# Modulation vectors in four column tiles of the array, and the first gate's products beside the first attention's preparation

## The chip, the cores and the metric

The kernel runs on one core of one Trainium2 chip. The metric is the time of one execution on the device in microseconds (us), the median of the runs shown. A core has five engines with a queue each: TensorE (PE in the profile, its weight loads PEld), VectorE (DVE), ScalarE (ACT), GpSimd (POOL) and SyncE (SP, which here only issues DMAs). Each engine works through its own list in order; semaphores make one wait for another.

## The reference, cut to what matters

Two blocks work on 1024 tokens and 256 context tokens of 1024 channels. Each layer is modulated by vectors that are computed from one conditioning vector `c` (for the tokens) and one `c_ctx` (for the context). The first block has two layers, with three vectors of 1024 each; the second block one layer with six:

```
# first block, layer l
shift, scale, gate       = split(silu(c)     @ w_mod[l] + b_mod[l], 3)
shift_c, scale_c, gate_c = split(silu(c_ctx) @ w_mod[l] + b_mod[l], 3)
h = rms_norm(x, norm_w[l]) * (1 + scale) + shift        # hc alike, from the context
parts = split_in(h @ w_in[l])
... attention, short convolution, conformer branch -> y ...
x = x + gate * (y @ w_out[l])
# second block
sh1, sc1, g1, sh2, sc2, g2 = split(silu(c) @ ada_w + ada_b, 6)     # and the same with c_ctx
u = layernorm(x) * (1 + sc1) + sh1
... SSD, RWKV and GLA mixers, then a mixture of experts ...
```

So `scale` and `shift` are wanted before a layer begins, and the gates only at its output projection.

## The kernel before, in words

`gemv` (L149 to L169) computes one such product for both vectors at once. `cs` holds silu(c) and silu(c_ctx) as 128 x 8 x 2: eight slices of 128 channels, two columns each. The matrix is read in chunks of 128 columns: one DMA on SP's queue brings a chunk `gemv_w` of 1024 x 128 (512 KB) into one of four buffers (two in the RWKV loop). Eight matmuls (L159), one per slice, add up to a result of 2 x 128 in PSUM: `cs[:, kk]` (128x2) is the stationary operand and the chunk's slice (128x128) the moving one. They are in fp32, and each appears as two records in the trace, so a chunk has 16 records. After four chunks (a group; two in the RWKV loop) VectorE copies the row of 2 x 512 to SBUF (L163), TensorE turns each 128 columns of it into 128 x 2 by a transpose (L166), and VectorE adds the bias (L168). `gemv` is a generator: it yields after each chunk, so its callers can put pieces of it between other work.

There are 96 chunks. Four places run them:

- `begin` in `block1`: layer 0's modulation (24 chunks). It runs all of shift and scale (16 chunks, four groups) and then `g` = (1 + scale) * norm_w (L398, L399). Then it goes through ten token tiles: `put_h` transposes a normalised tile (L248), scales and shifts it (L253 on VectorE, L256 on ScalarE) and splits it into two parts `hh` (L258) and `hl` (L259), two halves for each tile. After each tile one chunk of the gate runs (`run(gv, 1)`). The input projection (`product`, L104 to L106, three matmuls for each weight and token slice) follows.
- `second`, which `attention` of layer 0 gets as its `side`: layer 1's modulation (24 chunks). `beside(main, side, n)` runs `n` pieces of the side for each step of the main work, here while the first pair of heads is prepared: `prepare` (products, norms with a power on GpSimd at L87 and L847), `turn` (transposes of keys and queries, L876) and `maxima` (scores, L891, and their row maxima, L892 to L900). `run(side)` then finishes what is left of the side, and the attention's own first scores follow.
- the side of layer 1's attention: the second block's shift and scale (16 chunks of `ada_w`).
- the RWKV loop of the second block: the other 32 chunks of `ada_w`, with `group=2` and two buffers of `gemv_w`; there the PSUM tag `gv` has one bank, which the product and the transposes share.

The order of the instructions on each engine is fixed when the kernel is built, by a scheduler that goes by the program's order and the pools' free buffers. So an instruction of TensorE that waits holds up all that stands behind it on that engine.

The experts' loop at the end gathers rows by indices `ix`, of which the pool holds eight buffers, one for each block in flight.

Of the kernel before, what the change touches and what calls it, by code (L numbers as in the profile page):

```python
# [20 lines left out]
P = 128  # L21
# [18 lines left out]
class K:  # L40


    def __init__(self, ctx, tc):
# [12 lines left out]
        nc.vector.memset(ones, 1.0)  # L56
        self.ones = ones
        self.mhalf = self.const.tile([P, 1], F32, name="mhalf")
        nc.vector.memset(self.mhalf, -0.5)
# [84 lines left out]
def vec(ap):  # L144

    return ap.rearrange("(n p) -> n p", p=P)


def gemv(k, pool, out, cs, w, b, ncols, chunk=128, group=4, tag="mm", ttag="tr", bufs=4):  # L149

    nc = k.nc
    for g0 in range(0, ncols, chunk * group):
        ps = k.bank(tag=tag)
        n = min(chunk * group, ncols - g0)
        for c0 in range(0, n, chunk):
            wt = pool.tile([P, KD, chunk], F32, name="gemv_w", tag="gemv_w", bufs=bufs)
            k.load(wt, w[:, g0 + c0:g0 + c0 + chunk].rearrange("(k p) n -> p k n", p=P))
            for kk in range(KD):
                nc.tensor.matmul(ps[:2, c0:c0 + chunk], cs[:, kk], wt[:, kk], start=kk == 0, stop=kk == KD - 1)  # L159
            if c0 + chunk < n:  # L160
                yield
        row = pool.tile([2, chunk * group], F32, name="gemv_r", tag="gemv_r", bufs=2)
        nc.vector.tensor_copy(row[:, :n], ps[:2, :n])  # L163
        pt = k.bank(tag=ttag)
        for j in range(n // P):
            nc.tensor.transpose(pt[:, 2 * j:2 * j + 2], row[:, j * P:(j + 1) * P], k.ident[:2, :2])  # L166
        j0, nj = g0 // P, n // P
        nc.vector.tensor_tensor(out[:, j0:j0 + nj, :], pt[:, :2 * nj].rearrange("p (j s) -> p j s", s=2),  # L168
                                b[:, j0:j0 + nj].unsqueeze(2).to_broadcast([P, nj, 2]), op=OP.add)  # L169
        yield  # L170
# [153 lines left out]
def mod_vectors(k, pool, name, cvec, cctx):  # L324
    v = k.vectors(pool, name, [("c", vec(cvec)), ("cc", vec(cctx))])
    cs = pool.tile([P, KD, 2], F32, name=name + "_cs")
    sg = pool.tile([P, KD, 2], F32, name=name + "_sg")
    for s, key in enumerate(("c", "cc")):
        nc = k.nc
        nc.scalar.activation(sg[:, :, s], v[key], AF.Sigmoid)  # L330
        nc.vector.tensor_tensor(cs[:, :, s], sg[:, :, s], v[key], op=OP.mult)
    return cs


def block1(k, I, x_open, x_out, ahead, fill):
# [5 lines left out]
    with ExitStack() as es:  # L341
# [25 lines left out]
        def vectors(l):  # L367
# [20 lines left out]
            layer.append((v, hw, tabs))  # L388

        def modulation(l, gp, **kw):  # L390

# [3 lines left out]
            mods.append((m, g))  # L395
            n = 2 * KD
            yield from gemv(k, gp, m, cs, I["w_mod"][l], v["bmod"], 2 * D, **kw)
            nc.vector.tensor_scalar(g, m[:, KD:2 * KD], 1.0, None, op0=OP.add)  # L398
            nc.vector.tensor_tensor(g, g, v["norm"].unsqueeze(2).to_broadcast([P, KD, 2]), op=OP.mult)  # L399
            yield  # L400
            yield from gemv(k, gp, m[:, n:], cs, I["w_mod"][l][:, 2 * D:], v["bmod"][:, n:], D, **kw)

        def second(gp, **kw):

            vectors(1)
            yield from modulation(1, gp, **kw)

        hstack = ExitStack()
# [9 lines left out]
        def begin(wp):  # L418
# [15 lines left out]
            xs = [ready(t) for t in range(before)]  # L434
            run(gv, 2 * KD + 1 - 4)
            m, g = mods[0]
            for t in range(NT):
                s = 1 if t < CT else 0
                put_h(k, wp, xs[t], t, h[0], h[1], g[:, :, s], m[:, :KD, s])
                if t + before < NT:  # L440
                    xs.append(ready(t + before))
                run(gv, 1)
            run(gv)

# [708 lines left out]
class Mixer:  # L1153
# [1357 lines left out]
    def moe(self, xp, raw, late, finish):  # L2511
        k, nc, tc, I = self.k, self.nc, self.tc, self.I
        A = nc.vector
        with ExitStack() as es:
# [34 lines left out]
            def gather(st, pc, base):  # L2549
# [12 lines left out]
                A.scalar_tensor_tensor(c[:n, 0:1], c[:n, 2:3], slot[:n, 0:1], c[:n, 0:1], op0=OP.mult, op1=OP.add)  # L2562
                st.ix = xp.tile([P, 1], I32, name="ix", bufs=8)
                A.tensor_tensor(st.ix[:n], c[:n, 0:1], slot[:n, 1:2], op=OP.add)
# [342 lines left out]
```

## Time and profile before

| | us |
|---|---|
| median of 3 runs (4383.2 to 4387.87) | 4385.77 |
| profiled execution | 4396.88 |
| its span | 4394.7 |
| TensorE busy in it | 4042.7 (92%) |
| VectorE busy | 2889.0 (66%) |
| ScalarE busy | 1992.9 (45%) |
| GpSimd busy | 1172.9 (27%) |

The profile is of one execution. Busy time adds the records of an engine, and overlapping ones count once; matmuls are pipelined, so the mean of one record is longer than the distance from one start to the next. The clock granted to TensorE is 0.953 of full speed as a mean over the span. DMA moved 558.8 MB, at a mean of 127 GB/s.

### The profile page before, as it was taken

The page shows a single profiled execution, that of the slowest core. Times are in us where ns is not written, and L with a number is a line of the kernel's source. Part 1 is how long each engine was busy: PE and PEld are TensorE (multiplying, and loading weights), DVE is VectorE, ACT ScalarE, POOL GpSimd, SP SyncE. Part 2 cuts the span into 40 slices and gives each one's busy share as a digit, 9 for nine tenths or more (in the row PEclk, how much of TensorE's full clock was granted, in tenths as well). Part 3 has the DMA queues.
Part 4 walks back from the last instruction along what each step waited for, and adds up shares of the span by engine and source line. Part 5 has one row for each costly group of instructions (what it writes and reads, how often), then busy time and mean ns, then how long its engine had stood idle before and what let it go on. Part 6 is the DMA issues. An engine that isn't in the chain of part 4 may idle for free. (4 is left out here: it accounts for less than half of the span.)

```text
span 4394.7 us, 61923 instructions
## 1 busy us (share of the span) xinstructions
PE 4042.7 (92%) x22376; PEld 3080.2 (70%) x22376; DVE 2889.0 (66%) x5659; ACT 1992.9 (45%) x4292; POOL 1172.9 (27%) x1211
## 2 busy tenths in 40 slices
PE   8999899999998999999997999999999899899993
PEld 5787666667776666688786688777777666666662
DVE  4683577764745777645765555567878777777774
ACT  4122366653112666423353132434246666666664
POOL 1200133332101333321333331123312233222333
PEclk9999899999999999999997999799999999999996
DMA  6121400123123001334444410215359788888885
GB/s 187 34 64 41 126 13 13 30 80 107 44 63 106 8 13 37 110 121 127 125 126 137 123 34 27 83 34 173 113 211 300 249 274 270 259 264 260 272 264 166
DMA packets 371315, 558.80 MB, mean 127 GB/s; under 512 B 52126, under 2 KB 285056, under 8 KB 346048
## 3 DMA queue, kind: packets, MB, share of 16 engines
q1 hardware_dynamic: 335728, 432.81, 30.7%
q0 software_dynamic: 35280, 122.02, 10.7%
q8 instruction: 177, 2.90, 0.3%
q14 instruction: 130, 1.06, 0.1%
HBM read 438.42 MB, written 116.33 MB: 126 GB/s over the span
## 5 line engine op out<-in xcount | busy, mean ns | idle before, releaser
L95 DVE TENSOR_TENSOR wa_lo<-w_raw,wa_hi 128x512 fp32r<-128x512 f32 x520 | 340.2, 687 | 53.6 <-ACT wa_hi L94 51.0
L94 ACT ACTIVATE wa_hi<-w_raw 128x512 fp32r<-128x512 f32 x520 | 303.3, 625 | 90.8 <-PE mm L106 49.0
L104 PE MATMUL mm<-hh,w_hi 128*128 128x512 f32 (+1 forms) x848 | 319.3, 377 | 4.7 <-ACT h L256 4.7
L105 PE MATMUL mm<-hl,w_hi 128*128 128x512 f32 (+1 forms) x848 | 318.2, 375 | 0.0
L106 PE MATMUL mm<-hh,w_lo 128*128 128x512 f32 (+1 forms) x848 | 316.4, 373 | 0.0
L892 DVE TENSOR_REDUCE mx<-mm 128x1 f32<-128x512 f32 (+1 forms) x400 | 225.0, 587 | 53.4 <-PE mm L891 50.9
L926 ACT ACTIVATE pe<-mm 128x512 f32<-128x512 f32 (+1 forms) x336 | 193.0, 588 | 144.8 <-PE mm L106 115.6
L104 PE MATMUL mm<-wa_hi,xh 128*128 128x512 f32 (+3 forms) x632 | 257.6, 408 | 0.0
L105 PE MATMUL mm<-wa_lo,xh 128*128 128x512 f32 (+3 forms) x632 | 251.7, 398 | 1.2 <-DVE wa_lo L95 1.2
L106 PE MATMUL mm<-wa_hi,xl 128*128 128x512 f32 (+3 forms) x632 | 250.7, 397 | 2.1 <-DVE xl L95 2.1
L931 POOL TENSOR_TENSOR pl<-pe,ph 128x512 fp32r<-128x512 f32 x96 | 142.1, 1482 | 335.3 <-ACT ph L930 328.5
L931 DVE TENSOR_TENSOR pl<-pe,ph 128x512 fp32r<-128x512 f32 (+1 forms) x240 | 204.2, 863 | 38.6 <-ACT ph L930 37.3
L2629 POOL DMA_INDIRECT acc_d<-y,ix x97 | 171.3, 1766 | 201.7 <-DMA acc_d<-y,ix 86.9
L159 PE MATMUL mm<-gemv_w,b_c_cs 128*2 128x128 f32 x1536 | 197.3, 284 | 8.8 <-DMA gemv_w<-in_w_mod_dram 5.6
L595 DVE SCALAR_TENSOR_TENSOR acc<-zc,b_v,acc 128x512 f32<-128x512 f32 (+1 forms) x300 | 199.2, 711 | 1.5
L2585 PE MATMUL mm<-ident,xg 128*128 128x128 f32 (+5 forms) x840 | 119.4, 288 | 85.0 <-DMA xg<-h_d,ix 85.0
L104 PEld LDWEIGHTS mm<-hh,w_hi 128*128 128x128 f32 x848 | 160.9, 190 | 39.9 <-issue 7.6
L104 PE MATMUL mm<-wb_hi,hidh 128*128 128x512 f32 (+5 forms) x420 | 188.8, 450 | 0.0
L2585 PEld LDWEIGHTS mm<-ident,xg 128*128 128x128 f32 (+5 forms) x840 | 109.1, 198 | 111.2 <-issue 99.1
L2574 POOL COPY wc<-xg 128x1 f32<-128x1 f32 (+5 forms) x97 | 44.0, 454 | 534.6 <-DMA xg<-h_d,ix 534.6
L105 PEld LDWEIGHTS mm<-hl,w_hi 128*128 128x128 f32 x848 | 161.2, 190 | 34.3 <-issue 7.6
L94 ACT ACTIVATE w_hi<-w_raw 128x1024 fp32r<-128x1024 f32 x61 | 64.6, 1059 | 262.4 <-PE mm L105 227.6
(780 smaller groups left out, 11637.5 us busy)
## 6 DMA issues: line engine op xcount, KB each, us to landing
w_raw<-in_exp_w_dram SPq DMA_DIRECT2D x192, 1024.0 KB
w_raw<-in_w_in_dram SPq DMA_DIRECT2D x69, 512.0 KB
gemv_w<-in_w_mod_dram SPq DMA_DIRECT2D x48, 512.0 KB
gemv_w<-in_ada_w_dram SPq DMA_DIRECT2D x48, 512.0 KB
rec<-rec SPq DMA_DIRECT2D x64, 256.0 KB
wo_raw<-in_w_out_dram SPq DMA_DIRECT2D x20, 512.0 KB
y<-ydram SPq DMA_DIRECT2D x36, 256.0 KB
xt<-in_x_dram SPq DMA_DIRECT2D x16, 512.0 KB
```

What stands on the lines that cost most here:

```text
L94: nc.scalar.activation(hi, src, AF.Copy)
L95: eng.tensor_tensor(lo, src, f32(hi), op=OP.subtract)
L104: mm(out, ah, bh, start=start, stop=False)
L105: mm(out, ah, bl, start=False, stop=False)
L106: mm(out, al, bh, start=False, stop=stop)
L159: nc.tensor.matmul(ps[:2, c0:c0 + chunk], cs[:, kk], wt[:, kk], start=kk == 0, stop=kk == KD - 1)
L595: nc.vector.scalar_tensor_tensor(o, zc[:, ft, p0 + j:p0 + j + c[1]], v["cfw"][:, 2 * j + ft:2 * j + ft + 1], o, op0=OP.mult, op1=OP.add)
L892: nc.vector.tensor_reduce(mx[:, t, c:c + 1], ps[:, :n], axis=AX.X, op=OP.max)
L926: nc.scalar.activation(pe, ps, AF.Exp)
L931: (nc.gpsimd if j % PLP == PLP - 1 else nc.vector).tensor_tensor(pl, pe, f32(ph), op=OP.subtract)
L2585: nc.tensor.transpose(ps[:, j * n:(j + 1) * n], xk[:, 4 * q + j], k.ident[:n, :n])
L2629: nc.gpsimd.indirect_dma_start(out=self.acc_d, out_offset=bass.IndirectOffsetOnAxis(ap=st.ix[:n, 0:1], axis=0), in_=y[:n], in_offset=None, ...
```

## The change

The changed `gemv` widens the stationary operand. `gemv_c` is a zeroed tile of 128 x 8 x 32 with `cs` in its first two columns of each slice, made once per call. The eight matmuls of a chunk go to four column tiles of the array: slice `kk` writes to PSUM partitions 32 (kk mod 4) and up, so each tile adds up two slices, and the sum of the four tiles is still to be made. The row that VectorE copies now has 128 partitions (32 for each tile, two of them not zero) and one buffer in place of two. In place of each transpose four matmuls have 32 columns of that row as the stationary operand and `quads`, a constant of 128 x 2 with ones at the two rows of each tile, as the moving one: they sum the four tiles and turn the row at once, each into a column tile of its own.

The gate of layer 0 leaves `begin`; `second` runs it ahead of layer 1's vectors and modulation. So `begin` runs 16 chunks, and the side of the first attention 32. The buffers of `ix` are seven in place of eight.

```diff
+        self.quads = self.const.tile([P, 2], F32, name="quads")
+        nc.vector.tensor_reduce(self.quads, self.ident.rearrange("p (q s) -> p s q", q=4)[:, :2], axis=AX.X, op=OP.add)
...
     nc = k.nc
+    wide = pool.tile([P, KD, 32], F32, name="gemv_c", tag="gemv_c", bufs=1)
+    nc.vector.memset(wide, 0.0)
+    nc.vector.tensor_copy(wide[:, :, :2], cs)
...
             for kk in range(KD):
-                nc.tensor.matmul(ps[:2, c0:c0 + chunk], cs[:, kk], wt[:, kk], start=kk == 0, stop=kk == KD - 1)
+                q = slice(kk % 4 * 32, kk % 4 * 32 + 32)
+                nc.tensor.matmul(ps[q, c0:c0 + chunk], wide[:, kk], wt[:, kk], start=kk < 4, stop=kk >= KD - 4)
...
-        row = pool.tile([2, chunk * group], F32, name="gemv_r", tag="gemv_r", bufs=2)
-        nc.vector.tensor_copy(row[:, :n], ps[:2, :n])
+        row = pool.tile([P, chunk * group], F32, name="gemv_r", tag="gemv_r", bufs=1)
+        nc.vector.tensor_copy(row[:, :n], ps[:, :n])
         pt = k.bank(tag=ttag)
         for j in range(n // P):
-            nc.tensor.transpose(pt[:, 2 * j:2 * j + 2], row[:, j * P:(j + 1) * P], k.ident[:2, :2])
+            for q in range(0, P, 32):
+                nc.tensor.matmul(pt[q:q + 32, 2 * j:2 * j + 2], row[:, j * P + q:j * P + q + 32], k.quads, start=True,
+                                 stop=True)
...
-            n = 2 * KD
             yield from gemv(k, gp, m, cs, I["w_mod"][l], v["bmod"], 2 * D, **kw)
...
             yield
-            yield from gemv(k, gp, m[:, n:], cs, I["w_mod"][l][:, 2 * D:], v["bmod"][:, n:], D, **kw)
+
+        def gate(l, gp, **kw):
+            yield from gemv(k, gp, mods[l][0][:, n:], cs, I["w_mod"][l][:, 2 * D:], bmod[l][:, n:], D, **kw)
 
         def second(gp, **kw):
 
+            yield from gate(0, gp, **kw)
             vectors(1)
             yield from modulation(1, gp, **kw)
+            yield from gate(1, gp, **kw)
...
-            run(gv, 2 * KD + 1 - 4)
+            run(gv)
...
-                run(gv, 1)
-            run(gv)
...
-                st.ix = xp.tile([P, 1], I32, name="ix", bufs=8)
+                st.ix = xp.tile([P, 1], I32, name="ix", bufs=7)
```

In the changed kernel the matmuls of `gemv` are on L167 and the sums on L175, the transposes of `put_h` on L258, and the products on L107 to L109. TensorE at the start, before; a row here is one or more like instructions in a run, and shapes are those of the output:

```order
L159 MATMUL mm<-gemv_w,b_c_cs 2x128 x32
L166 MATMUL mm<-ident,gemv_r 128x2 x4
L159 MATMUL mm<-gemv_w,b_c_cs 2x128 x10
L248 MATMUL mm<-ident,xn 128x128 x4
L159 MATMUL mm<-gemv_w,b_c_cs 2x128 x2
L248 MATMUL mm<-ident,xn 128x128 x4
L159 MATMUL mm<-gemv_w,b_c_cs 2x128 x9
L248 MATMUL mm<-ident,xn 128x128 x4
```

And of the change, from the same place on:

```order
L167 MATMUL mm<-gemv_w,gemv_c 32x128 x32
L175 MATMUL mm<-quads,gemv_r 32x2 x16
L258 MATMUL mm<-ident,xn 128x128 x12
L107 MATMUL mm<-hh_154,w_hi 128x256 x2
L108 MATMUL mm<-hl_155,w_hi 128x256
```

The gate's matmuls no longer lie between the transposes of the token tiles, and the first products follow at once.

TensorE at the end of the first attention's preparation, before (L891 are the scores of the maxima, L900 turns a tile's maxima, L104 to L106 with `qh` are the attention's first scores):

```order
L891 MATMUL mm<-kh_3426,qh_3424 128x256
L159 MATMUL mm<-gemv_w,b_c_cs 2x128 x5
L900 MATMUL mm<-nident,mx 1x128
L159 MATMUL mm<-gemv_w,b_c_cs 2x128 x4
L166 MATMUL mm<-ident,gemv_r 128x2 x4
L104 MATMUL mm<-qh_3424,kh_3426 128x256
```

And of the change:

```order
L906 MATMUL mm<-kh_3381,qh_3379 128x256
L915 MATMUL mm<-nident,mx 1x128
L167 MATMUL mm<-gemv_w,gemv_c 32x128 x32
L175 MATMUL mm<-quads,gemv_r 32x2 x16
L167 MATMUL mm<-gemv_w,gemv_c 32x128 x32
L175 MATMUL mm<-quads,gemv_r 32x2 x16
L107 MATMUL mm<-qh_3379,kh_3381 128x256
```

Before, the last chunks lie between the maxima; in the change the last two groups (x32 is four chunks) stand together behind all of them, ahead of the first scores.

TensorE in the RWKV loop, before (the other lines are steps of one RWKV item):

```order
L159 MATMUL mm<-gemv_w,b_c_cs 2x128 x16
L1676 MATMUL mm<-vtm,M 128x64
L1716 MATMUL mm<-bc,U 128x128
L1718 MATMUL mm<-U,bc 128x128
L1719 MATMUL mm<-vtm,bc 128x128
L166 MATMUL mm<-ident,gemv_r 128x2 x2
L1687 MATMUL mm<-R,XD_21432 128x128 x2
```

And of the change, at the same steps:

```order
L167 MATMUL mm<-gemv_w,gemv_c 32x128 x8
L1691 MATMUL mm<-vtm,M 128x64
L1731 MATMUL mm<-bc,U 128x128
L1733 MATMUL mm<-U,bc 128x128
L1734 MATMUL mm<-vtm,bc 128x128
L175 MATMUL mm<-quads,gemv_r 32x2 x8
L1702 MATMUL mm<-R,XD_21641 128x128 x2
L1731 MATMUL mm<-bc,U 128x128
L1733 MATMUL mm<-U,bc 128x128
L167 MATMUL mm<-gemv_w,gemv_c 32x128 x8
```

Before, a whole group of two chunks (x16) stands in one place; in the change its two chunks stand apart, with steps of the item between them, so that the 32 chunks spread over about six items instead of about three. In all, the changed order of TensorE has 78 runs of L167. On SP's queue at the start the first load of the input projection's weights (`w_raw`) stood behind 4 loads of `gemv_w` and the next two behind 24; now all three stand behind 16.

## Rows read from the trace of the kernel before

**Rows 1.** The page, busy us, share of the span, instructions:

```profile
PE 4042.7 (92%) x22376; PEld 3080.2 (70%) x22376; DVE 2889.0 (66%) x5659; ACT 1992.9 (45%) x4292; POOL 1172.9 (27%) x1211
```

**Rows 2.** Line L159, whole span: durations ns min/median/max, first and last start:

```profile
L159 PE MATMUL mm<-gemv_w,b_c_cs x1536: 269/273/421, 18.1 to 2520.1; 128*2 128x128 f32 x192
```

**Rows 3.** Timeline of TensorE around 490 us: start, us, engine, line, count, wait:

```profile
480.57 0.59 PE L166 MATMUL mm<-ident,gemv_r 2*128 2x2 f32 x4 [8.69 <-DVE gemv_r L163]
481.09 8.82 PE L159 MATMUL mm<-gemv_w,b_c_cs 128*2 128x128 f32 x64
489.84 1.08 PE L876 MATMUL mm<-ident,k__3444 128*96 128x128 f32 x8
490.85 0.40 PE L166 MATMUL mm<-ident,gemv_r 2*128 2x2 f32 x4
491.18 7.15 PE L159 MATMUL mm<-gemv_w,b_c_cs 128*2 128x128 f32 x64
```

**Rows 4.** Windows at the start: PE, PEld, DVE, ACT, POOL, clock, DMA, GB/s:

```profile
30.00:40.00 10.00, 8.73 (x77) 6.07 (x76) 1.43 (x2) 0.00 (x0) 0.74 (x2) 1.00 1.16 292
...
80.00:90.00 10.00, 10.00 (x72) 8.27 (x70) 9.35 (x23) 9.24 (x23) 1.48 (x4) 1.00 0.38 106
```

**Rows 5.** Timeline of all engines, end of the first 16 chunks:

```profile
57.93 1.37 DVE L253 TENSOR_SCALAR h<-mm,b_g,b_m 128x128 f32<-128x128 f32 x4
...
77.36 0.39 PE L104 MATMUL mm<-hh,w_hi 128*128 128x256 f32 x1
```

**Rows 6.** Line L259, halves of put_h:

```profile
L259 DVE TENSOR_TENSOR hl<-h,hh x20: 670/682/693, 60.4 to 100.8; 128x512 fp32r<-128x512 f32 x20
```

**Rows 7.** Window in the first preparation:

```profile
470.00:480.00 10.00, 1.88 (x18) 1.25 (x15) 2.83 (x11) 1.81 (x9) 7.51 (x3) 0.72 0.38 106
```

**Rows 8.** Timeline of the maxima (VectorE), and of the first scores (TensorE):

```profile
506.45 1.72 DVE L892 TENSOR_REDUCE mx<-mm 128x1 f32<-128x512 f32 x3 [0.79 <-PE mm L891]
...
508.92 1.73 DVE L892 TENSOR_REDUCE mx<-mm 128x1 f32<-128x512 f32 x3 [0.56 <-PE mm L891]
...
527.63 0.39 PE L104 MATMUL mm<-qh,kh 97*128 97x256 f32 x1
```

**Rows 9.** Line L159 in the second preparation:

```profile
L159 PE MATMUL mm<-gemv_w,b_c_cs x256: 271/273/418, 1376.5 to 1434.8; 128*2 128x128 f32 x128
```

**Rows 10.** Timeline of TensorE ahead of the second turn:

```profile
1396.56 0.59 PE L166 MATMUL mm<-ident,gemv_r 2*128 2x2 f32 x4 [4.12 <-DVE gemv_r L163]
1397.07 4.85 PE L159 MATMUL mm<-gemv_w,b_c_cs 128*2 128x128 f32 x22
```

**Rows 11.** Line L159 in the RWKV loop after 2420, and its waits for loads:

```profile
L159 PE MATMUL mm<-gemv_w,b_c_cs x416: 269/273/417, 2422.3 to 2520.1; 128*2 128x128 f32 x139
...
  DMA gemv_w<-in_ada_w_dram: 5.9, 8
```

**Rows 12.** Windows in the RWKV loop and behind it:

```profile
2410.00:2420.00 10.00, 2.63 (x17) 2.30 (x16) 4.50 (x4) 3.22 (x6) 5.78 (x3) 0.65 0.36 97
...
2470.00:2480.00 10.00, 10.00 (x84) 7.89 (x82) 3.46 (x9) 2.42 (x4) 1.72 (x2) 1.00 0.64 182
...
2520.00:2620.00 100.00, 99.33 (x697) 83.85 (x694) 56.91 (x135) 34.32 (x92) 33.20 (x40) 1.00 0.12 32
```

**Rows 13.** Timeline of TensorE around L1531, four column tiles:

```profile
2023.34 0.39 PE L105 MATMUL mm<-b_hl,w_hi 128*128 128x512 f32 x1
2023.56 0.39 PE L106 MATMUL mm<-b_hh,w_lo 128*128 128x512 f32 x1
2023.88 0.38 PE L1531 MATMUL mm<-rec 64*32 64x32 f32 x32
2024.19 0.50 PE L104 MATMUL mm<-b_hh,w_hi 128*128 128x512 f32 x1
2024.53 0.39 PE L105 MATMUL mm<-b_hl,w_hi 128*128 128x512 f32 x1
```

**Rows 14.** Loads of gemv_w in the first preparation, on SP:

```profile
L77 SPq DMA_DIRECT2D gemv_w<-in_w_mod_dram x24: 367/368/1836, 440.9 to 512.4; - x24
```

More of the change, by code (lines that the diff above doesn't have):

```diff
@@ L325, in mod_vectors @@
     v = k.vectors(pool, name, [("c", vec(cvec)), ("cc", vec(cctx))])
+    nc = k.nc
     cs = pool.tile([P, KD, 2], F32, name=name + "_cs")
@@ L328, in mod_vectors @@
     for s, key in enumerate(("c", "cc")):
-        nc = k.nc
         nc.scalar.activation(sg[:, :, s], v[key], AF.Sigmoid)
@@ L388, in vectors @@
             layer.append((v, hw, tabs))
+        n = 2 * KD
+        bmod = []
         def modulation(l, gp, **kw):
@@ L395, in modulation @@
             mods.append((m, g))
-            n = 2 * KD
+            bmod.append(v["bmod"])
             yield from gemv(k, gp, m, cs, I["w_mod"][l], v["bmod"], 2 * D, **kw)
```

## The prediction, made before the changed kernel ran

> **What bounds the kernel now.** I read the page's busy shares first [rows 1], then for each stretch in which the matrix-vector products (`gemv`) run its line in the trace, its timeline and its windows. TensorE is busy 4042.7 of 4394.7 us [rows 1]. L159, the products with a moving 128x128 tile, has 1536 records [rows 2]. These overlap: 64 of them take 7.15 us [rows 3], so one costs about 0.109 us and a chunk (8 matmuls, 16 records) 1.75 us; where the clock is low, 64 take 8.82 us [rows 3]. The kernel has 96 chunks, about 168 us of TensorE. The question is how much of it stands in the way in each of four stretches, since 92% over all says nothing on that.
>
> *Start, 0 to 101 us.* Between 30 and 40 us TensorE is 8.73 of 10 busy and the DMA engines are full: a share of 1.16 at 292 GB/s [rows 4]. The first 16 chunks end at 57 us, and `put_h` starts its first tile at 57.93 [rows 5]. Its 20 halves end from 60.4 to 100.8 us [rows 6], 2.13 us each; ScalarE and VectorE are busy 9.24 and 9.35 of 10 at 80 to 90 [rows 4]. The 8 gate chunks lie between the transposes, and the first product of the input projection begins only at 77.36 [rows 5].
>
> *First attention's preparation, 440 to 528 us.* TensorE is 1.88 of 10 busy at 470 to 480, where GpSimd is busy 7.51 with the powers of the norms [rows 7]; it waits 8.69 us at L166 for a copy that VectorE makes only after them [rows 3]. Then 64 records of `gemv` (8.82 us) stand ahead of the turn of the keys at 489.84 and 64 more (7.15) ahead of its rest [rows 3]. The maxima go at 2.47 us a tile (506.45 to 508.92), of which VectorE's large reductions need 1.73 [rows 8].
>
> *Second preparation, about 1370 to 1437.* The same with 16 chunks, from 1376.5 to 1434.8 [rows 9]; 22 records take 4.85 us at a low clock ahead of the turn [rows 10].
>
> *RWKV loop, 2378 to 2521.* 32 chunks; 416 of their records lie after 2420 [rows 11]. There TensorE is mostly 9 to 10 of 10 busy, and from 2520 on 99.33 of 100 [rows 12], so time freed there carries on. Before 2420 it waits on chains (2.63 of 10 at 2410 to 2420 [rows 12]).
>
> **Whether four column tiles run at once.** The trace has one such product. L1531 writes its output in four column tiles of 32, all from the same 64 rows, in fp32. 32 records start within 0.31 us (2023.88 to the next start at 2024.19 [rows 13]), 9.7 ns each. One after the other they would need, scaled from 0.109 us for 128 columns, 27 ns each, 0.87 us in all. So they overlap at least 2.8 times. So scaled, a chunk costs between 0.44 us (four at once) and 0.62 (2.8 times); I take 0.5, since these short records carry their start-up. The saving is 1.25 us per chunk, 120 us over 96.
>
> The Trainium skill, "TensorE: Matmul & The Clock Gate", Packing small matmuls, has matmuls of different tiles overlap, but a weight load overlap a running matmul only where the row groups differ. The tiles here share all their rows, so by that rule the chunk would stay near its 1.75 us and the sum come out as in rival 3. The trace speaks against it: in rows 13 the tiles share their rows too.
>
> *The switch.* L106 to L1531 is 0.32 us where L105 to L106 is 0.22, and L104 to L105 behind it is 0.34 [rows 13]: about 0.2 us in and out together. The new order has 78 runs of tiled products, so 0 to 16 us; many lie in idle time, and the old products broke the stream as well. I take 4. The Trainium skill's "TensorEngine Tiling (Array Packing)", Key Properties, says that a change of the tiling mode drains TensorE; the 0.2 us agree with a short drain, and by that rule the whole 16 would be paid, a sum of 44 instead of 56.
>
> **The change part by part.**
>
> Start. Removed from TensorE: 1.25 x 16 = 20 us before `put_h`; what is late next is the DMA. After the first product at 18.1 us [rows 2] some 12 loads of 512 KB and 3 rows of x remain, 15 x 1.8 us (512 KB at 292 GB/s [rows 4]) = 27, so the last weights land at about 44 to 45; with the copy, the sums and `g` the first tile starts at about 46 instead of 57.9: 12 us. On SP's queue the first `w_raw` is now behind all 16 loads, not 4; it lands at about 50, with its split behind it, near the first h at 52. The gate's 8 chunks leave too (14 us between 59 and 77), but `put_h` is bound by ScalarE and VectorE, so I add only 1; products that start earlier could gain up to 8. **13, between 6 and 20.**
>
> First preparation. It gets 8 chunks more, 32. From TensorE go 24 x 1.75 = 42 us, 32 x 0.5 = 16 come. Up to 470 about 7 chunks lie between the products: 9 us earlier. The power chain stays. The 16 us ahead of and within the turn shrink to 5 or 6: the turn ends at about 480, not 500. The maxima then need 2.0 to 2.4 us a tile, to about 503. But the order of TensorE has the last 8 chunks behind all maxima and in front of the attention's first scores; four of their loads can start only when the four ahead have been used (four buffers): 4 x 1.8 + about 2 us until landing = 9, and copies and sums 3. The loads alone are 32 x 1.8 = 58 us from 440.9 [rows 14], 499 at the earliest. I put the first scores at 518 instead of 527.63 [rows 8]: **9, between -2 and 20.** At the lower end the queue is fed no faster than before (23 loads issued over 71.5 us, 3.1 each [rows 14]), less the tenth that the shorter chunks free: 440.9 + 31 x 2.8 = 528, plus 2 for the last.
>
> Second preparation. 16 chunks x 1.25 = 20 us. Those before the turn lie partly in the wait of L166 (4.12 us [rows 10]), and the maxima are soon bound by VectorE, as above: some 8 are lost. There is no tail, since 16 loads (29 us) end within the maxima. **12, between 5 and 18.**
>
> RWKV loop. 416 records are 26 chunks, 26 x 1.25 = 32 us where TensorE is the bound, and some 2 us of the 6 chunks before. Against it: two buffers. TensorE waits 5.9 us for loads there now [rows 11]; after the change a buffer is refilled in about 1.8 + 2 us, and the new order has a chunk after about every 2 us of other work, so it is just fed; I take 7 us of new waits. One bank holds both the product and the sums, so each group waits for copy and sum before the next; the order puts other rows between. **27, between 5 and 38.**
>
> Nothing: clearing and filling `gemv_c` (six times, each under 1 us of VectorE, going by 0.6 for 128x512 [rows 8], ahead of loads that take longer); `quads`, once; 16 sums (32 records, 0.31 us as in rows 13) for 4 transposes (0.33 between starts [rows 3]); the copy, 128 rows for 2 at the same 512 columns; seven `ix` buffers, with seven blocks of the experts between uses of one. Were these covers gone: 32 groups x 0.5 us of VectorE, 16 us; I keep 5 in the range.
>
> Clock: next to TensorE's idle stretches the rows show a granted 0.72 [rows 7] and 0.65 [rows 12]. A gap of 9 us ahead of the attention could put some us behind it at half speed, as could the loop's waits. I take 1 off and keep 8 in the range.
>
> **Sum.** 13 + 9 + 12 + 27 - 4 - 1 = 56. The profiled execution took 4396.9 us (2.2 beyond its span), 11.1 above the median of 4385.8. 4396.9 - 56 = 4341, which in runs like the median is about **4330 us**. The lower ends (6 - 2 + 5 + 5 = 14, less 16 of switches, 8 of clock and 5 of covers) give a loss of 15; that all come at once is unlikely. The upper ends give 96, 4290.
>
> **Rivals.**
> 1. *The loads set the pace.* For it: the DMA's share at the start [rows 4], the two buffers of the loop, the tail. Against it: the DMA's share of 0.64 in the loop's window [rows 12]. Start 10, first preparation 0, second 10, loop 10, less 5: 25, so 4361.
> 2. *TensorE carries nearly all of it on*, as it is 92% busy: 120 less some 25 in idle time, 4291. For it: 99% after 2520 [rows 12]; against it: `put_h`, the power chain and the tail.
> 3. *Slower: tiles that share the array's rows take turns*, each load behind the running matmul. Place: every chunk. Then a chunk stays at 1.75 us; the start gains 0 to 5 from the gate's leaving, and the first preparation pays 8 x 1.75 = 14 and the tail of 9, less 6 that fall into the idle time before the turn; with 78 switches at 0.1: 14 + 9 - 6 + 8 - 5 = 20 slower, 4406. It decides from a chunk of about 1.4 us on. Against it: rows 13.
> 4. *The change does little*: a chunk at 1.4 us. The four stretches' 61 shrink by 0.35 / 1.25 to 17, less the 14 of the gate's chunks, which no longer hide: 3, so 4383.
>
> **How the numbers follow.** Forecast (4305 to 4350) 0.53; rival 1 0.22; rival 2 0.15; rival 3 0.05; rival 4 0.05. A measurement of this kernel can tell about 0.2%, 8.8 us, from no change. Faster: 0.53 + 0.22 + 0.15 + 0.01 = 0.91; same 0.05 (rival 4 and the far end of rival 1); slower 0.04. The range from 4287 to 4370 takes in the first three, less their far ends.
>
> **What would show it.** A chunk's 16 records start within 0.4 to 0.65 us (over 1.4: rival 3). The first tile of `put_h` comes at 44 to 48 us. The first scores come some 9 us earlier, counted from the first of the stretch's loads, with a wait for `gemv_w` just ahead of them. The second preparation's products take some 12 us less than their 58. The loop has few waits for `gemv_w`; many would be rival 1. The copy of 128 rows takes the time of 2. The prediction is wrong if the chunk is short and the gain still under 30 us: then the time freed was not TensorE's to give.

## The result, and the profile after

The changed kernel takes 4330.99 us (median of 4 runs, 4321.92 to 4346.18) against 4384.49 for the kernel before beside it: a ratio of 0.9891, 95% interval 0.9845 to 0.9938. The profiled execution has a span of 4344.4 us, 50.3 below that of before; it is the slowest of the four (4346.18), 15 us above their median, as that of before lay 11 above its own.

The page's busy line, as in [rows 1], and line L167, which stands where L159 stood [rows 2]:

```profile
PE 3970.7 (91%) x23047; PEld 3033.1 (70%) x23048; DVE 2888.9 (66%) x5672; ACT 1993.5 (46%) x4292; POOL 1175.7 (27%) x1211
```

```profile
L167 PE MATMUL mm<-gemv_w,gemv_c x1536: 269/297/424, 18.5 to 2483.8; 128*32 128x128 f32 x192
```

TensorE lost 72 us of busy time and has as many records of `gemv` as before. A chunk in the RWKV loop, and what follows it (timeline of TensorE):

```profile
2441.07 0.65 PE L167 MATMUL mm<-gemv_w,gemv_c 128*32 128x128 f32 x16
2441.64 1.30 PE L1971 MATMUL mm<-aq,kz 128*128 128x128 f32 x8
2442.89 0.65 PE L167 MATMUL mm<-gemv_w,gemv_c 128*32 128x128 f32 x16
2443.46 0.49 PE L1971 MATMUL mm<-aq,kz 128*128 128x128 f32 x2
```

What counts is the distance from a chunk's start to the next instruction: 0.57 us for 16 records, at a granted clock of 1.00. Before, 64 took 7.15 us to the end of the last one [rows 3], from start to start about 1.75 per 16. Two chunks that follow each other, in the first preparation:

```profile
458.31 1.08 PE L167 MATMUL mm<-gemv_w,gemv_c 128*32 128x128 f32 x32
```

The last record is 0.28 long, so 31 starts lie in 0.80 us, 0.41 per chunk.

Where the 50.3 us came from is read from the same instruction in both traces. Stretches in us, before and after:

| stretch | before | after | gained | predicted |
|---|---|---|---|---|
| start of the program to the first `q` of the first preparation (L815, now L830) | 440.2 | 435.7 | 4.5 | 13 |
| from there to the first exponential of the attention (L926, now L941) | 88.1 | 79.3 | 8.8 | 9 |
| last `put_h` of layer 1 to the table load of its attention | 356.0 | 350.3 | 5.7 | 12 |
| first to last L1665 (now L1680) of the RWKV loop | 589.8 | 560.6 | 29.2 | 27 |
| all the rest | 2920.6 | 2918.5 | 2.1 | - |

Each row is one execution against one. How far one can stray, the runs of the next section show for the loop: it takes 549.1 to 560.6 us in nine traces with the change's chunk (the one here is the longest), and 581.0 to 589.8 in three whose chunk takes 1.75 to 1.80 us (before, e1, e5; the one here is again the longest).

**The start.** The changed kernel's first tile of `put_h`, its first product, the halves of `put_h`, and two windows (columns as in [rows 4]), which answer to [rows 4 to 6]:

```profile
52.69 1.37 DVE L263 TENSOR_SCALAR h<-mm,b_g,b_m 128x128 f32<-128x128 f32 x4
...
59.25 0.58 PE L107 MATMUL mm<-hh,w_hi 128*128 128x256 f32 x1 [0.44 <-ACT hh L268]
```

```profile
L269 DVE TENSOR_TENSOR hl<-h,hh x20: 670/684/694, 55.2 to 99.7; 128x512 fp32r<-128x512 f32 x20
```

```profile
30.00:40.00 10.00, 5.83 (x112) 3.39 (x112) 1.61 (x3) 1.01 (x2) 0.74 (x2) 0.50 1.16 291
...
70.00:80.00 10.00, 5.50 (x29) 3.35 (x28) 8.01 (x19) 9.33 (x24) 3.43 (x8) 0.81 0.34 110
```

The first tile comes 5.2 us earlier, the last half only 1.1 earlier: the 20 halves now take 44.5 us from first to last, 40.4 before. At 30 to 40 us the granted clock is 0.50, the lower of its two levels. From the last half to the first instruction of the convolution behind it (L595 at 150.5 us before, L610 at 145.3 in the change) are 49.7 us before and 45.6 now, and TensorE is busy in all of it. So of the lead that arrives there, 5.2 us, 1.1 come from `put_h` and 4.1 from what stands behind it: 229 records of TensorE where there were 246, since the products began at 59.25 and not at 77.36 [rows 5].

**The first preparation.** TensorE behind the maxima (L915 is the last step of a tile's maxima, L107 the first scores), for [rows 8]:

```profile
500.08 0.59 PE L915 MATMUL mm<-nident,mx 128*1 128x128 f32 x2 [0.89 <-DVE mx L909]
500.31 3.24 PE L167 MATMUL mm<-gemv_w,gemv_c 128*32 128x128 f32 x64
504.33 0.43 PE L175 MATMUL mm<-quads,gemv_r 128*32 128x2 f32 x32 [0.78 <-DVE gemv_r L171]
506.67 1.08 PE L167 MATMUL mm<-gemv_w,gemv_c 128*32 128x128 f32 x16 [1.90 <-DMA gemv_w<-in_w_mod_dram]
508.33 1.08 PE L167 MATMUL mm<-gemv_w,gemv_c 128*32 128x128 f32 x16 [0.58 <-DMA gemv_w<-in_w_mod_dram]
510.03 1.08 PE L167 MATMUL mm<-gemv_w,gemv_c 128*32 128x128 f32 x16 [0.62 <-DMA gemv_w<-in_w_mod_dram]
511.54 1.08 PE L167 MATMUL mm<-gemv_w,gemv_c 128*32 128x128 f32 x16 [0.43 <-DMA gemv_w<-in_w_mod_dram]
513.43 0.60 PE L175 MATMUL mm<-quads,gemv_r 128*32 128x2 f32 x32 [0.81 <-DVE gemv_r L171]
513.96 0.58 PE L107 MATMUL mm<-qh,kh 97*128 97x256 f32 x1
```

The maxima end at 500.1, some 24 us earlier than before (64.4 us after the stretch's first `q`), and 13.9 us lie between their last step and the first scores: four chunks that wait for nothing, and four that wait for their loads, one by one, 1.5 to 1.7 us apart.

**The second preparation.** Two windows of the changed kernel, in its maxima (1393.4 to 1415.7):

```profile
1400.00:1410.00 10.00, 9.20 (x81) 5.19 (x73) 6.09 (x13) 0.59 (x1) 0.00 (x0) 0.50 0.01 2
1410.00:1420.00 10.00, 9.62 (x24) 4.91 (x24) 6.01 (x16) 2.65 (x4) 0.00 (x0) 0.50 0.00 0
```

TensorE is busy 9.2 and 9.6 of 10 at a clock of 0.50; before, the maxima had 1.00:

```profile
1420.00:1430.00 10.00, 10.00 (x69) 5.29 (x67) 8.03 (x18) 0.59 (x1) 0.00 (x0) 1.00 0.25 72
```

**The RWKV loop.** L1680 in the changed kernel, and the waits of L167 for loads in the loop, for [rows 11]:

```profile
L1680 PE MATMUL mm<-rec x320: 272/376/792, 2327.9 to 2888.5; 64*128 64x256 f32 x128, 64*128 64x128 f32 x32
```

```profile
  DMA gemv_w<-in_ada_w_dram: 6.3, 10
```

### The profile page after: what moved, and what is told of

Its sections match the earlier page's. It is cut to its first block, busy times and chain, and to the rows that moved or that the text cites. A ratio compares the mean times of both kernels' runs of the same rounds, so it can differ in the third digit from the quotient of the medians.

```text
span 4344.4 us, 63290 instructions
## 1 busy us (share of the span) xinstructions
PE 3970.7 (91%) x23047; PEld 3033.1 (70%) x23048; DVE 2888.9 (66%) x5672; ACT 1993.5 (46%) x4292; POOL 1175.7 (27%) x1211
## 5 line engine op out<-in xcount | busy, mean ns | idle before, releaser
L107 PE MATMUL mm<-hh,w_hi 128*128 128x512 f32 (+1 forms) x848 | 320.7, 379 | 4.1 <-ACT h L266 3.3
L109 PE MATMUL mm<-hh,w_lo 128*128 128x512 f32 (+1 forms) x848 | 318.0, 375 | 0.0
L941 ACT ACTIVATE pe<-mm 128x512 f32<-128x512 f32 (+1 forms) x336 | 193.3, 588 | 153.4 <-PE mm L109 124.7
L907 DVE TENSOR_REDUCE mx<-mm 128x1 f32<-128x512 f32 (+1 forms) x400 | 224.3, 587 | 51.6 <-PE mm L906 49.3
L107 PE MATMUL mm<-wa_hi,xh 128*128 128x512 f32 (+3 forms) x632 | 257.6, 408 | 0.5 <-ACT xh L97 0.5
L109 PE MATMUL mm<-wa_hi,xl 128*128 128x512 f32 (+3 forms) x632 | 250.2, 396 | 0.0
L946 POOL TENSOR_TENSOR pl<-pe,ph 128x512 fp32r<-128x512 f32 x96 | 142.6, 1487 | 333.0 <-ACT ph L945 326.1
L610 DVE SCALAR_TENSOR_TENSOR acc<-zc,b_v,acc 128x512 f32<-128x512 f32 (+1 forms) x300 | 199.3, 712 | 1.5
L107 PEld LDWEIGHTS mm<-hh,w_hi 128*128 128x128 f32 x848 | 162.0, 191 | 40.1 <-issue 7.4
L107 PE MATMUL mm<-wb_hi,hidh 128*128 128x512 f32 (+5 forms) x420 | 186.8, 445 | 0.0
L109 PEld LDWEIGHTS mm<-hh,w_lo 128*128 128x128 f32 x848 | 162.2, 191 | 28.8 <-issue 1.3
```

The source lines that it names most:

```text
L107: mm(out, ah, bh, start=start, stop=False)
L109: mm(out, al, bh, start=False, stop=stop)
L610: nc.vector.scalar_tensor_tensor(o, zc[:, ft, p0 + j:p0 + j + c[1]], v["cfw"][:, 2 * j + ft:2 * j + ft + 1], o, op0=OP.mult, op1=OP.add)
L907: nc.vector.tensor_reduce(mx[:, t, c:c + 1], ps[:, :n], axis=AX.X, op=OP.max)
L941: nc.scalar.activation(pe, ps, AF.Exp)
L946: (nc.gpsimd if j % PLP == PLP - 1 else nc.vector).tensor_tensor(pl, pe, f32(ph), op=OP.subtract)
```

## The experiments

Two theories stood against each other on the gain that the start and the second preparation did not give. *Clock:* a TensorE with less to do is granted half its clock, and the freed time is given back in slow matmuls. *Bounds:* the loads, VectorE, ScalarE and the order set those stretches, and TensorE's time was not what counted. A third question was whether the column tiles make the gain at all. The stretches in the text are those of the table; "the change" is the changed kernel.

**e1: the gate's move alone.**

```diff
-def gemv(...)     # four column tiles
+def gemv(...)     # as before: stationary cs[:, kk], transposes
```

> Only the move of layer 0's gate (and the seven ix buffers); gemv is that of the kernel before, one row of 2 columns. If the column tiles carry the gain, this run shows none: a chunk stays at 16 records in 1.75 us, the start gains 0 to 6 us, the first preparation pays 8 chunks (14 us) and a tail of 9 to 14 us of loads behind the maxima: 4390 to 4405 us in all. If moving the gate carries a good part of it, the time is below 4375.

4394.28 us against 4384.37, ratio 1.0015 (1.000 to 1.003). The start is 441.4 us, the first preparation 104.9, 16.8 longer than before; behind the maxima stand two groups of 7.15 us each. None of the gain comes from the move; in the first preparation it costs time where a chunk is long.

**e2: the column tiles alone.**

```diff
-            yield from gate(0, gp, **kw)          # in second
+            run(gv, 1)                            # in begin, behind each put_h, as before
```

> Only the column tiles; layer 0's gate stays in the start, one chunk behind each token tile, 24 chunks in the first preparation. If the 13.7 us that the change spends behind the maxima of the first preparation come from the eight more loads, the preparation is 10 to 13 us shorter than in the change; the start is the same within 3 us when TensorE has room there (a chunk is half a microsecond), so 4317 to 4323 us. If the gate's loads hold up the first weights of the input projection (eight loads of 1.8 us), the start is some 8 to 12 us later than in the change and the two cancel: about 4330.

4325.52 us, ratio 0.9864 (0.9837 to 0.9890). The second expectation came: the first preparation takes 69.6 us, 9.7 less than in the change, and the start 444.8, 9.1 more, with the input projection's first weights issued at 68.9 us (46.7 in the change). The two cancel within the intervals. The move of the gate is worth nothing either way, once a chunk is short.

**e3: TensorE kept busy in the start.**

```diff
-            for kk in range(KD):
+            for kk in list(range(KD)) * 3:        # in begin only
```

> As the change, but in the start alone every chunk's eight matmuls are issued three times (each time the sum begins anew, so the last one counts): about 1.4 us of TensorE per chunk instead of 0.5, no other difference. If the start gained only 4.5 us because TensorE, with little to do, was granted half its clock (0.50 from 30 to 60 us) and then did the transposes and first products slowly, the clock stays near 1.00 here, the halves of put_h end at 94 to 97 us instead of 99.7, and the first preparation begins 3 to 6 us earlier (435.7 in the change): about 4326. If the start is bound by the loads, ScalarE and VectorE alone, the clock rises and the preparation begins within 1 us of 435.7.

4330.79 us, ratio 0.9890 (0.9853 to 0.9927). The clock rose to 0.72 to 1.00 between 30 and 60 us, and the start became longer, 439.5 us, with the first tile at 58.4. By itself that does not settle it, since the added matmuls also put the first tile 5.7 us later. Runs whose start is the change's own do. In the next one, e4, the profile shows 1.00 from 30 to 60 us,

```profile
30.00:40.00 10.00, 5.83 (x112) 3.40 (x112) 1.61 (x3) 0.50 (x2) 0.74 (x2) 1.00 1.18 291
40.00:50.00 10.00, 6.24 (x120) 3.79 (x124) 0.86 (x2) 0.00 (x0) 0.00 (x0) 1.00 1.16 315
```

and the first tile comes at 52.9, the preparation begins at 434.6. In e7, at 1.00 too, they come at 53.1 and 436.3; at 0.50, in the change, e8 and e11, at 52.7 to 53.7 and 435.7 to 436.6. A clock twice as high is worth about 1 us at most: the clock theory fails for the start.

**e4: the side's pieces earlier in the first preparation.**

```diff
-RS = ((.75, 0, .5), (.25, 1, .5))
+RS = ((1.0, 0, .6), (.25, 1, .5))
```

> As the change, but the side's pieces in the first preparation come faster (1.0 per step of its products instead of 0.75, 0.6 per step of the maxima instead of 0.5), so that the order has no group of chunks left behind the maxima. If the tail (maxima end at 500.1, first scores at about 514) was a matter of order, the first scores come 8 to 12 us earlier: about 4320. If the loads set the pace (32 of 1.8 us from 441: 499, and four buffers), the same waits move into the maxima, and it gains 0 to 4 us.

4327.88 us, ratio 0.9869 (0.9841 to 0.9896). The first preparation takes 72.5 us, 6.8 less. The end of it (TensorE):

```profile
502.75 0.65 PE L167 MATMUL mm<-gemv_w,gemv_c 128*32 128x128 f32 x16
503.53 0.38 PE L915 MATMUL mm<-nident,mx 128*1 128x128 f32 x2
504.46 0.64 PE L167 MATMUL mm<-gemv_w,gemv_c 128*32 128x128 f32 x16 [0.55 <-DMA gemv_w<-in_w_mod_dram]
506.05 0.43 PE L175 MATMUL mm<-quads,gemv_r 128*32 128x2 f32 x32 [0.94 <-DVE gemv_r L171]
506.41 0.39 PE L107 MATMUL mm<-qh,kh 97*128 97x256 f32 x1
```

The last step of the maxima is at 503.53 and the first scores at 506.41: a tail of 2.9 us, while the maxima end 3.5 later than in the change. So about half of the tail's 13.9 us was order: it lies between the two expectations. TensorE's waits for loads in the stretch fall only from 11.7 to 8.7 us; what else makes the maxima longer was not tried apart.

**e5 and e6: one column tile, two column tiles.**

```diff
-                q = slice(kk % 4 * 32, kk % 4 * 32 + 32)
+                q = slice(0, 32)                              # e5
+                q = slice(kk % 2 * 32, kk % 2 * 32 + 32)      # e6
```

with the row copied from 32 or 64 partitions and `start` and `stop` to match.

> As the change, but all eight matmuls of a chunk go to one column tile: the stationary operand is still 32 columns wide, the row is copied from 32 partitions and turned by matmuls with the constant, only nothing can run side by side. If the tiles' running at once is the gain, a chunk's 16 records start over 1.7 to 1.8 us again and the time is that of the gate's move alone, 4385 to 4400, with the RWKV loop as long as before (590 us from the first to the last L1665) or some us shorter. If the new sums in place of the transposes, or the one buffer of the row, gave a good part in the loop, the loop is under 575 us here.

> As the change, but with two column tiles in place of four. If a chunk's time goes with the number of tiles, its 16 records start over 0.85 to 0.95 us, that is 0.85 of 1.75 saved against 1.2 to 1.3: two thirds of the gain where TensorE is the bound. RWKV loop about 565 to 570 us, 4345 to 4355 us in all. If the loads or the chains bound the loop by then, it is no longer than in the change (549 to 561) and the time within 5 us of the change.

TensorE in the loop, first with one tile, then with two:

```profile
2453.17 3.68 PE L167 MATMUL mm<-gemv_w,gemv_c 128*32 128x128 f32 x32
2456.78 1.13 PE L1942 MATMUL mm<-vt,kd 128*128 128x256 f32 x4
...
2459.76 1.94 PE L167 MATMUL mm<-gemv_w,gemv_c 128*32 128x128 f32 x16
```

```profile
2440.76 1.07 PE L167 MATMUL mm<-gemv_w,gemv_c 128*32 128x128 f32 x16
2441.76 0.93 PE L1971 MATMUL mm<-aq,kz 128*128 128x128 f32 x6
```

32 records in 3.61 us with one tile (1.80 per chunk), 16 in 1.00 with two, 0.57 with four. One tile: 4395.86 us, ratio 1.0041 (1.0020 to 1.0062), the loop 584.0. Two: 4344.65, 0.9929 (0.9900 to 0.9957), the loop 570.4. The wider stationary operand, the sums in place of the transposes and the single buffer of the row give nothing by themselves (the loop with one tile lies between the 581.0 of e1 and the 589.8 of before); that tiles run at once gives all of it, and the loop follows the chunk. The scheduler also orders the loop's chunks anew when they are short: with one tile several stand two and two, as before, with two or four tiles mostly one by one. So e6 against the change compares tiles at nearly one order; in e5 the two are not apart. The second preparation does not follow the chunk: 344.7 us with two tiles, 350.3 with four (see e7).

**e7: TensorE kept busy in both preparations.**

```diff
+            for kk in list(range(KD)) * 3:        # in the two preparations only
```

> As the change, but in the two attention preparations every chunk's matmuls are issued three times (each time the sum begins anew): about 1.4 us of TensorE per chunk. In the second preparation of the change the maxima ran at a granted clock of 0.50 with TensorE 9.2 to 9.6 of 10 busy. If the lower clock of a less busy TensorE is what took back gain there, the clock is near 1.00 here and the second preparation (from the last put_h of layer 1, 1067.3, to the table load at 1417.6: 350.3 us) is 3 to 6 us shorter, in spite of 14 us more of matmuls. If it is the VectorE and the loads that bound it, or if the work of the matmuls costs what it gives back, it is the same or up to 8 us longer, and the first preparation too.

4359.91 us, ratio 0.9969 (0.9952 to 0.9986). The second preparation takes 357.2 us, 6.9 more than in the change, the first 100.1, 20.8 more. The clock is 1.00 in the second's maxima, which take 20.7 us, 1.6 less than in the change; but they begin 7.5 us later after the last `put_h`: the work costs more than it returns. That does not say that the clock is free. Five traces have the change's second preparation and reach it alike: in all of them it is 326.0 to 326.1 us from the last `put_h` to the first reduction of the maxima. From there to the last one it is 22.3 and 22.2 us in the change and e11, at a mean granted clock of 0.58, and 18.2, 18.2 and 18.1 in e2, e3 and e9, at 0.89. The change, then e2 (columns as in [rows 4]):

```profile
1393.40:1415.70 22.30, 20.28 (x163) 10.39 (x164) 15.82 (x38) 0.59 (x1) 0.00 (x0) 0.58 0.18 51
```

```profile
1392.60:1410.80 18.20, 15.50 (x163) 8.02 (x164) 15.73 (x38) 0.59 (x1) 0.00 (x0) 0.89 0.22 63
```

Two more agree: e4, whose edit does not touch this stretch, takes 23.2 us at 0.56 (after 323.0), and e6, with two tiles, 18.5 at 1.00. So 4 of the 6 us that are missing there are the clock, by comparing runs of like instructions and not by an edit.

**e8: eight buffers in the preparations.**

```diff
-tag="gv", ttag="gv")
+tag="gv", ttag="gv", bufs=8)
```

> As the change, but with eight buffers of weights in place of four in the two preparations, in the same order. If the tail behind the maxima (500.1 to 514) is made by the four buffers, all eight last chunks are loaded by the time the maxima end, the wait for loads there goes (11.7 us of waits in the stretch now) and the first scores come 8 to 10 us earlier: about 4321. If the DMA queues are full anyway (32 loads of 1.8 us from 441 on: 499), it gains 3 to 6 us.

4328.33 us, ratio 0.9893 (0.9871 to 0.9915). The first preparation takes 77.9 us, 1.4 less. Behind the maxima no chunk waits for a load any more, and the tail falls to 7 us; but the maxima end 6.5 later, at 506.6, with their last steps at half clock. That is less than either expectation: more buffers alone hardly shorten it.

**e9: the first block's `c` first.**

```diff
-        self.cs = mod_vectors(k, mp, "b2_c", ...)      # when the second block is set up
+        def vecs(self): ...                            # the same, called behind the start's first four chunks
```

> As the change, but the first block's c is turned first and the second block's vectors (c, ada_b, mu and the rest) are loaded and turned behind the first four chunks. In the change TensorE's first gemv waits until 18.5 us behind those vectors, and the DMA engines are idle from 12 to 18 us since all four buffers are full. If the start is set by the chain of loads, gemv begins near 5 us, the last weights land some 8 to 10 us earlier, the first tile of put_h starts at 42 to 45 us instead of 52.7 and the first preparation 5 to 9 us earlier than 435.7: about 4323. If put_h and the products behind it (ScalarE, VectorE, the order) are the bound, the first tile comes earlier but the preparation begins within 2 us of 435.7.

4330.60 us, ratio 0.9882 (0.9856 to 0.9908). `gemv` began at 5.58 us and the first tile only at 51.6, the preparation at 434.4. So it does not test an earlier first tile; the expectation missed what stands on SP's queue. In the change the loads are issued so (SP, start and time of the issue):

```profile
17.56 0.29 SPq L80 DMA_DIRECT2D b_bm_st<-in_norm_w_dram  x1
...
19.69 0.40 SPq L80 DMA_DIRECT2D gemv_w<-in_w_mod_dram  x1
21.16 0.25 SPq L80 DMA_DIRECT2D b_v_st<-in_q_norm_w_dram  x1
...
24.86 0.23 SPq L80 DMA_DIRECT2D b_v_st<-in_cf_conv_w_dram  x1
25.19 0.35 SPq L80 DMA_DIRECT2D xt<-in_x_dram  x1
25.59 5.73 SPq L80 DMA_DIRECT2D gemv_w<-in_w_mod_dram  x4
```

The fifth load of weights is issued at 19.69, the other eleven only from 25.59 on, behind the small vectors; in e9 ten of them from 26.00 on. The eleven issues follow each other every 1.74 us until 44.7 (the line above ends with its window), and the last chunk starts at 49.50.

**e10: the three edits together** (e4, e8, e9).

> The change with the three edits together: first block's c first, the side's pieces faster in the first preparation (no tail behind its maxima) and eight buffers of weights in the preparations. If their gains add up (5 to 9, 7, and 1 to 3 us), about 4313, some 15 to 18 below the change; if the earlier start is given back before the preparation, about 4321.

4317.12 us (4298.44 to 4335.11), ratio 0.9852 (0.9827 to 0.9876); the start 435.3, the first preparation 75.7, the second 342.6. The gains did not add up: the start's was given back, and the first preparation is 3.2 us longer than in e4, though the tail is gone here too and TensorE waits 3.5 us for loads. The interval overlaps that of the change.

**e11: half the bytes in the RWKV loop.**

```diff
-            k.load(wt, w[:, ...])
+            k.load(wt[:, :4], w[:4 * P, ...])     # and matmuls on wt[:, kk % 4]; in the loop only
```

> As the change, but in the RWKV loop each chunk's load brings only the first four of the eight slices (256 KB), and the matmuls use those twice, so the second block's gates are not the reference's; the same matmuls, half the bytes. If the two buffers' loads still bound the loop, its length (first to last L1665, 549 to 561 in the runs of the change's loop so far) falls to 543 to 548. If TensorE, the chains and VectorE set it, it stays within 549 to 561.

The loop takes 562.5 us in the one trace: no shorter, though TensorE's waits for loads in it fall from 6.3 to 2.9 us. The loads do not bound it. The total (4362.57) isn't compared: the second block's values are other ones, and the time behind the loop is 41 us longer (other values can send other tokens to the experts; that this is the reason is not shown).

**e12: the start's weights ahead of all other vectors**, on e10.

```diff
-            run(gv, 4); rope_in(); vectors(0); late()
+            run(gv, 12)       # rope_in and vectors(0) behind the second put_h, late() behind the sixth
```

> As e10_best, but the start's 16 chunks of weights and the first three token tiles stand ahead of all other vectors on SP's queue (the vectors of layer 0 are loaded behind the second tile of put_h, those of the second block behind the sixth). In e9 and e10 eleven or ten of the 16 loads were issued only from 26 us on, behind some twenty small loads of vectors. If that queue set the start, the 16 loads follow each other at 1.75 us from 1.5 us on, the last weights land at about 34 to 36, the first tile of put_h starts at 37 to 41 us instead of 51.8 and the first preparation begins at 427 to 431 instead of 435.3: about 4311. If put_h and the products behind it give the time back (put_h took 47 us from its first to its last half in the change, 43 before), the first tile comes as early, and the preparation still begins between 433 and 437: about 4317.

4318.44 us (4307.47 to 4323.95), ratio 0.9861 (0.9840 to 0.9882). The first tile starts at 40.8 us, 11 earlier than in e10, and the preparation at 434.1, 1.2 earlier. So the loads set the first tile, as expected, and most of its lead is lost before the preparation. What comes between is the convolution of the conformer branch on VectorE (L595 before, L610 in the change, L613 here):

```profile
L595 DVE SCALAR_TENSOR_TENSOR acc<-zc,b_v,acc x180: 462/743/1574, 150.5 to 299.5; 128x512 f32<-128x512 f32 x120, 128x256 f32<-128x256 f32 x60
```

```profile
L610 DVE SCALAR_TENSOR_TENSOR acc<-zc,b_v,acc x180: 462/745/1577, 145.3 to 294.1; 128x512 f32<-128x512 f32 x120, 128x256 f32<-128x256 f32 x60
```

It takes 148 to 151 us in all fourteen traces and begins at 150.5 before, at 145.3 in the change and at 143.2 in e12. From its begin to the preparation it is 289.7 to 291.4 us in all of them, so the lead at its begin is the lead at the preparation, within 2 us. The 17 us that the first tile gained in e12 over the kernel before were down to 7 by then. From the last half of `put_h` to the convolution it is 45.5 to 45.6 us in eleven traces whose gate has left the start, 46.4 in e12, 49.7 before and 56.3 in e2: the lead is lost within `put_h`. The edit also put the input projection's first weights later, at 49.0 us (46.7 in the change); the first product came at 58.1 (59.25), and `put_h` took 56 us (47); which of these gives the time back was not tried apart.

## Why the prediction was right, point by point

The time came where the sum put it, 4331 against 4330. Not all its terms did, and that the two agree so closely is luck: the four stretches were to give 61 us and gave 48.2 in the profiled pair. The 5 us taken off, 2.1 from the rest, and an execution of the change further above its median than that of before make up most of the difference.

*The chunk.* Predicted 0.5 us, between 0.44 and 0.62; measured 0.57 alone and less in a run of several. Right, and for the reason given: L1531 [rows 13] was the same thing in small. e5, e6 and the change show 1.80, 1.00 and 0.57 for one, two and four tiles. Rival 3 is out, and so is rival 4, with its chunk of 1.4 us. What a chunk without overlap costs shows in e5, 4396 where rival 3 said 4406, and in e1, 4394. Of the two rules weighed, that of the Trainium skill's "TensorE: Matmul & The Clock Gate", Packing small matmuls, on weight loads of tiles that share rows is not borne out by these runs; that of its "TensorEngine Tiling (Array Packing)", Key Properties, agrees with a drain that is short. The switch costs about 0.16 us, 0.57 for a lone chunk against 0.41 for one of two, so the 78 runs would cost 12 us if all were on the path. How many are no run shows, and the 4 us stay an estimate.

*The start: 13 predicted, 4.5 measured, outside its range of 6 to 20.* The step that failed is "After the first product at 18.1 us some 12 loads of 512 KB and 3 rows of x remain ..., so the last weights land at about 44 to 45". The loads do follow at 1.75 us each, but eleven of them are issued only from 25.6 on. I had the queue's order and counted bytes, not the some twenty small loads of vectors that stand ahead of them, each with its issue and some with a wait ahead of it. From 19.69 to 25.59, with eight of them and a row of x, that is 5.9 us, of 6.7 that the first tile came late (52.7 for 46). And the step from the first tile to the end of the stretch was wrong too: of a lead of 5.2 us at the first tile, `put_h` left 1.1, and with the first tile 5 us earlier than I wanted it (e12) the stretch gains 6, not 13. The other 4.1 us at the convolution go with the products that start earlier, which I put at 1, with up to 8.

*The first preparation: 9 predicted, 8.8 measured.* The last chunks behind the maxima, the four loads that can't start before, the 9 us of them: as predicted in kind (13.9 with the sums and the first four chunks, 12 predicted). The maxima ended 64.4 us after the stretch's begin, 62.8 predicted (503 less 440.2). But 503 and 12 make 515, and I put 518 with no term for the 3 us between: the longer maxima and tail used them up, so the 8.8 owe something to luck. e2 shows its other side: without the eight chunks it is 9.7 shorter.

*The second: 12 predicted, 5.7 measured, 10 in e2, e3 and e9.* The mechanism held; the size was off by the clock of the maxima (e7), 4 us, for which the sum took off 1 in all, with 8 in the range. The other 2 us are not accounted for.

*The loop: 27 predicted, 29.2 measured; 30 between the middle ones of the three long loops (584.0) and of the nine short ones (553.7).* Right in size. My two brakes were not what braked: waits for loads stayed (6.3 us, 5.9 before; 7 new ones predicted) and halving the bytes did not shorten the loop. What the term did not count are the waits for VectorE's copy ahead of the transposes (before) and the sums (the change), in the loop:

```profile
  DVE gemv_r L163: 33.4, 10
```

```profile
  DVE gemv_r L171: 17.4, 8
```

16 us went there in this pair, but the 33.4 is high: with a chunk that is not short the waits are 21.9 us in e1, 22.8 in e5 and 25.0 in e6, with the change's 9.7 to 19.8 in the nine traces. Part of them lies in stretches where TensorE waited for chains anyway; how much they add to the gain is not shown.

Of the terms put at nothing, the copy takes 0.55 us with 128 rows and 0.54 with 2 (medians), and clearing and filling `gemv_c` 0.27 and 0.17.

Rival 1 (the loads set the pace, 4361) held for the first tile of the start and for the tail, not for the end of the start or the loop. Rival 2 (nearly all of it carried on, 4291) is out; even with three more edits (e10) it is 4317.

## What to carry to other kernels

A matrix-vector product with a narrow stationary operand uses few columns of the array; padded to 32 and spread over four column tiles it ran three times as fast here, and the four partial sums came nearly for nothing in the matmuls that turned the row (32 records within 0.43 us, where four transposes took 0.40 [rows 3]). Count the gain only where TensorE ends the stretch: here nearly three fifths of it came from the one stretch that was TensorE's, and in the start neither a full clock nor earlier loads moved the end by more than 2 us (the latter in an edit that also put other loads later). On a queue that issues in order, small loads ahead of big ones cost their issue time and their staging buffers, and they show only in the queue's own timeline.

## What the runs showed of the hardware

- Four column tiles with 128 rows each run at once in fp32: 16 matmul records in 0.57 us, against 1.00 with two tiles and 1.80 with one.
- Executions of the same start ran from 30 to 60 us at a granted clock of 0.50 (the change, e8, e11) and of 1.00 (e4, e7), and the first tile came at 52.7 to 53.7 us in the ones, at 52.9 and 53.1 in the others: the level is not a matter of the program alone.
- The issue of a DMA of 1 KB takes SyncE 0.25 us, that of 512 KB 0.37 in the median of [rows 14], so twenty small ones cost a queue as much as thirteen large; eleven large ones in a row, at the start of the change, took 1.74 us each.
